# Copying the broadcast root of a norm out of PSUM, summing the last squares apart, and more side work beside the last groups of an FFN

## The chip, the cores and the metric

The kernel runs on one core of one Trainium2 chip. TensorE does the matrix products and writes PSUM banks; VectorE (DVE), ScalarE (ACT) and GpSimd (POOL) do elementwise work; SyncE (SP) issues transfers. The metric is device time in microseconds (us) for one execution. Median of three runs of the kernel before: 2212.97 us (2211.99 to 2215.68).

## The reference

One layer of a streaming encoder over 1024 prompt tokens and 32 sample tokens, width 1024: a gated FFN, two attention mixers, a second gated FFN, each with a norm before it (scaled and shifted) and a norm on its result.

```python
def rmsnorm(x, g):
    y = x * rsqrt(mean(x * x, axis=-1, keepdims=True) + EPS)
    return y * g
def adaln_in(x, g, shift, scale):
    return rmsnorm(x, g) * (1 + scale) + shift
def swiglu(h, w_gate, w_up, w_down):            # 1024 -> 2816 -> 1024
    return (silu(h @ w_gate) * (h @ w_up)) @ w_down
def layer(x, c, ...):
    h = adaln_in(x, gains[0], sh1, sc1)
    x = x + 0.5 * g1 * rmsnorm(swiglu(h, w1_gate, w1_up, w1_down), gains[1])
    h = adaln_in(x, gains[2], sh2, sc2)
    ...                                         # q, k, v = h @ w_in; two attention mixers
    o = concatenate([rmsnorm(oa, gg[:512]), rmsnorm(ob, gg[512:])]) @ w_out
    x = x + g2 * rmsnorm(o, gains[3])
    h = adaln_in(x, gains[4], sh3, sc3)
    x = x + 0.5 * g3 * rmsnorm(swiglu(h, w2_gate, w2_up, w2_down), gains[5])
```

## The kernel before, in words

Activations lie transposed: features on the 128 partitions (8 tiles k), tokens along the free axis, in three token blocks tb: 0 and 1 of 384 tokens, 2 of 256 + 32 = 288 (prompt and sample; scaled by separate coefficients, hence two operations, 256 and 32 wide, per tile). Each f32 product is three matmuls of split operands (`mm3`, L324 to L327: high by high, high by low, low by high), so a product over 8 tiles is 24 matmuls.

**FFN** (`ffn`). The 22 column tiles of the hidden width go in groups of two, x and y. For one block, `up(x)` makes `gate` and `up`, 24 matmuls each, in PSUM; ScalarE applies silu to gate (`sl`, L550), VectorE multiplies it with up (L551) and splits the product (`gg`, L553, L554); then `up(y)`, and `down` adds 4 × 12 `dn` matmuls to `facc`. gate, up, pv, pq and wo share a pool of three banks (`p1`). The first FFN (h1) runs all three blocks in every group but the last three, whose groups run blocks 0 and 1 first and then block 2 alone; the second (h3) begins with two groups of blocks 0 and 1, and then these two of block 2.

**Norm** (`mean_rstd`, `sumsq`). ScalarE squares two tiles at a time (`sq`, L364, four times); GpSimd folds the first two, VectorE the last two (L368, and L370 to add the earlier one); TensorE sums over partitions with `pss` matmuls (L357, one per 128 tokens, after the second and the fourth square); VectorE makes the root from pss (`rv`, `ry`, `rt`, L387 to L391 and L334 to L338, eleven to twelve small operations); TensorE spreads it over the partitions (`pr`, L405, one matmul per 128 tokens). pss and pr are handed out from one bank (`pc`) with other small things.

Two users: `resid` (L454) scales the sublayer's result by pr (L464, VectorE) and adds the old x, loaded as `xr` (L467); `norm_h` (L409) scales x by pr (`n`, L420, VectorE), adds the shift and splits it into `h_hi` (ScalarE, L444) and `h_lo` (L446 VectorE, L448 ScalarE with L449 GpSimd). `between` runs resid and then norm_h for one block. The norm of the mixers' output (`group_norm`) copies pr to SBUF (`rstd`, L1145) before it uses it.

**What sets the order.** These norms are generators in the list `side`; the FFN's `up` calls `step` after the gate's 24 matmuls and after up's 24, which runs some of their pieces in between (`PACE` = 2, in the first group `FAST` = 10). The program made so is then put in order by a list scheduler over all engines: an instruction is placed when its operands and its buffer are there, and each engine executes in the order given. Buffers are handed out in the order of the program. `rstd`, `sl` and a few more take the tag "s" (five buffers), `sq`, `n` and `xr` the tag "h" (five).

Of the kernel before, what the change touches and what calls it, by code (L numbers as in the profile page):

```python
# [33 lines left out]


PACE = 2
FAST = 10
OUTSTEP = 6
ABREAST = 1
# [35 lines left out]
def encoder_step(ctx: ExitStack, tc, x_prompt, x_sample, cache_a_k, cache_a_v, cache_b_k, cache_b_v,  # L75
# [30 lines left out]
    def s_tile(shape, name, dt=F32):  # L106
        return spool.tile(shape, dt, name=name, tag="s")
# [234 lines left out]
    def token_cols(w):  # L342
        return [(c, min(128, w - c)) for c in range(0, w, 128)]

    def sumsq(src, kts, w, bank, ends, fold=True):


        n = len(kts) // 2
        pss = bank("pss")
        cols = token_cols(w)  # L350
        behind = []

        def add_up(sq, first, last):
            halves = (0,) if fold else (0, 1)
            for q in halves:
                for j, (c0, m) in enumerate(cols):
                    te.matmul(pss[:m, j:j + 1], sq[:, q, c0:c0 + m], ones, start=first and j == 0 and q == 0,  # L357
                              stop=last and q == halves[-1], skip_group_check=True)

        acc, first = None, True  # L360
        for c in range(n):
            k = kts[2 * c]
            sq = h_tile([128, 2, 384], "sq")
            ae.activation(sq[:, :, :w], src[:, k:k + 2, :w], AF.Square)  # L364
            if fold:
                e = SQE[c % len(SQE)]
                e = ve if e == "v" else ge
                e.tensor_tensor(sq[:, 0, :w], sq[:, 0, :w], sq[:, 1, :w], op=OP.add)  # L368
                if acc is not None:
                    e.tensor_tensor(sq[:, 0, :w], sq[:, 0, :w], acc[:, 0, :w], op=OP.add)  # L370
                acc = sq
            if behind:
                add_up(*behind.pop())
            if c in ends or not fold:
                behind.append((sq, first, c == n - 1))
                acc, first = None, False
            yield
        add_up(*behind.pop())
        return pss

    def rstd_cols(pss, w, scale):
        cols = token_cols(w)
        v = small.tile([128, 4], F32, name="rv")
        m = cols[-1][1]
        nj = len(cols)
        if m < 128:
            ve.memset(v[:, nj - 1:nj], 1.0)  # L387
            ve.tensor_scalar(v[:, :nj - 1], pss[:, :nj - 1], scale, EPS, op0=OP.mult, op1=OP.add)
            ve.tensor_scalar(v[:m, nj - 1:nj], pss[:m, nj - 1:nj], scale, EPS, op0=OP.mult, op1=OP.add)
        else:  # L390
            ve.tensor_scalar(v[:, :nj], pss[:, :nj], scale, EPS, op0=OP.mult, op1=OP.add)  # L391
        return rsqrt(v[:, :nj], 128, nj)

    waits = [0]

    def mean_rstd(src, kts, w, scale, ends, bank=None):

        bank = bank or pc
        pss = yield from sumsq(src, kts, w, bank, ends)
        y = rstd_cols(pss, w, scale)  # L400
        for _ in range(waits[0]):
            yield
        pr = bank("pr")
        for j, (c0, m) in enumerate(token_cols(w)):
            te.matmul(pr[:, c0:c0 + m], y[:m, j:j + 1].to_broadcast([m, 128]), ident[:m, :m], start=True, stop=True)  # L405
        yield
        return pr

    def norm_h(x, tb, j, H, ahead=0):  # L409
        w = TB[tb][1]  # L410
        r = yield from mean_rstd(x, range(KT), w, 1.0 / D, JN)
        hi, lo = H[tb] = (u_tile(tb, "h_hi", F32R), u_tile(tb, "h_lo", F32R))

        def scaled(c, gated):
            n = h_tile([128, 2, 384], "n")
            if gated:
                for q in range(2):
                    k = 2 * c + q
                    for a, b, st in SEGS[tb]:
                        ve.scalar_tensor_tensor(n[:, q, a:b], x[:, k, a:b], acoef[:, j, st, k:k + 1], r[:, a:b],  # L420
                                                op0=OP.mult, op1=OP.mult)
            else:
                ve.tensor_tensor(n[:, :, :w], x[:, 2 * c:2 * c + 2, :w],
                                 r[:, None, :w].to_broadcast([128, 2, w]), op=OP.mult)
            return n

        ns = [scaled(c, False) for c in range(ahead)]
        if ns:
            yield "ahead"
        for c in range(KT // 2):  # L430
            n = ns[c] if ns else scaled(c, True)
            yield
            for q in range(2):
                k = 2 * c + q
                for a, b, st in SEGS[tb]:
                    sh = modT[:, st, 24 * j + k:24 * j + k + 1]
                    z = n[:, q, a:b]
                    if ns:
                        ac = acoef[:, j, st, k:k + 1]
                        ae.activation(hi[:, k, a:b], z, AF.Identity, bias=sh, scale=ac)  # L440
                        ve.tensor_scalar(z, z, ac, sh, op0=OP.mult, op1=OP.add)
                        (ge if q else ve).tensor_tensor(lo[:, k, a:b], z, hi[:, k, a:b], op=OP.subtract)
                    else:
                        ae.activation(hi[:, k, a:b], z, AF.Identity, bias=sh)  # L444
                        if k % 4 < 3:
                            ve.scalar_tensor_tensor(lo[:, k, a:b], z, sh, hi[:, k, a:b], op0=OP.add, op1=OP.subtract)  # L446
                        else:
                            ae.activation(z, z, AF.Identity, bias=sh)  # L448
                            ge.tensor_tensor(lo[:, k, a:b], z, hi[:, k, a:b], op=OP.subtract)  # L449
            yield  # L450
# [3 lines left out]
    def resid(f, tb, j):  # L454

        w = TB[tb][1]
        r = yield from mean_rstd(f, range(KT), w, 1.0 / D, JR)
        for c in range(KT // 2):
            s = slice(2 * c, 2 * c + 2)
            x = h_tile([128, 2, 384], "xr")  # L460
            dma.dma_start(x[:, :, :w], xs_dram[j][tb][:, s, :])
            for k in (2 * c, 2 * c + 1):
                for a, b, st in SEGS[tb]:
                    ve.scalar_tensor_tensor(f[:, k, a:b], f[:, k, a:b], gcoef[:, j, st, k:k + 1], r[:, a:b],  # L464
                                            op0=OP.mult, op1=OP.mult)
            yield
            (ge if c in POOL_ADDS else ve).tensor_tensor(f[:, s, :], f[:, s, :], x[:, :, :w], op=OP.add)  # L467
            yield
# [56 lines left out]
    def ffn(key, H, F, wg, wu, wd, per_group, key_out, after, beside=lambda ff, tb: None):  # L525
# [10 lines left out]
        for r, (gi, blocks) in enumerate(plan):  # L536
# [3 lines left out]
            def up(ff, tb):  # L540
                need((key, tb))
                w = TB[tb][1]
                hi, lo = H[tb]
                ps = [p1("gate"), p1("up")]
                for s in range(2):
                    for k in range(KT):
                        mm3(ps[s][:, :w], wgu[ff][s], k, hi[:, k, :], lo[:, k, :], k == 0, k == KT - 1)
                    step(FAST if gi == 0 else PACE)
                sl = s_tile([128, 384], "sl")
                ae.activation(sl[:, :w], ps[0][:, :w], AF.Silu)  # L550
                ve.tensor_tensor(sl[:, :w], sl[:, :w], ps[1][:, :w], op=OP.mult)  # L551
                g = g_tile([128, 2, 384], "gg", F32R)
                ae.activation(g[:, 0, :w], sl[:, :w], AF.Copy)  # L553
                ve.tensor_sub(g[:, 1, :w], sl[:, :w], g[:, 0, :w])  # L554
                gs[ff, tb] = g
                beside(ff, tb)
                if late:
                    late.pop()()
# [579 lines left out]
    def group_norm(tb, g):  # L1138
        w = TB[tb][1]
        if OH[tb] is None:  # L1140
            OH[tb] = (u_tile(tb, "o_hi", F32R), u_tile(tb, "o_lo", F32R))
        hi, lo = OH[tb]
        pr = yield from mean_rstd(O[tb], range(4 * g, 4 * g + 4), w, 2.0 / D, JG, p1)
        r = s_tile([128, 384], "rstd")
        ae.activation(r[:, :w], pr[:, :w], AF.Copy)  # L1145
        for c in range(2):
            z = h_tile([128, 2, 384], "z")
            for q in range(2):
                k = 4 * g + 2 * c + q
                ve.scalar_tensor_tensor(z[:, q, :w], O[tb][:, k, :], cst[:, 120 + k:121 + k], r[:, :w],  # L1150
                                        op0=OP.mult, op1=OP.mult)
            yield
            s = slice(4 * g + 2 * c, 4 * g + 2 * c + 2)
            ae.activation(hi[:, s, :], z[:, :, :w], AF.Copy)
            (ge if c in GNP else ve).tensor_tensor(lo[:, s, :], z[:, :, :w], hi[:, s, :], op=OP.subtract)
            yield
# [199 lines left out]
```

## Time and profile before

| | |
|---|---|
| median of the runs | 2212.97 us |
| the profiled execution | 2217.6 us, its span 2215.8 us, mean granted clock 0.984 |
| TensorE busy | 2161.6 us (98%) |
| VectorE, ScalarE, GpSimd busy | 1239.1 (56%), 697.8 (31%), 179.2 us (8%) |
| matmuls | 14012 |
| silu, `sl` (L550) | 132 operations, 60.9 us |
| copy of pr in the group norms (L1145) | 6 operations, 0.41 to 0.49 us each |

A row of a wait names the engine, what waited and for whom, then us in total, times and the longest. A row of a timeline has start, duration, engine, line, operation and, in brackets, the idle time just before and what ended it. A row of a stretch has its bounds, its length, the busy time and instructions (x) of each engine, the granted TensorE clock (1.00 is full), the share of the transfers and GB/s. Times are from the start of the span; the first FFN begins at 45, the work in front of the mixers at 831, the second FFN at 1414.

### The profile page before, as it was taken

The page shows a single profiled execution, that of the slowest core. Times are in us where ns is not written, and L with a number is a line of the kernel's source. Part 1 is how long each engine was busy: PE and PEld are TensorE (multiplying, and loading weights), DVE is VectorE, ACT ScalarE, POOL GpSimd, SP SyncE. Part 2 cuts the span into 40 slices and gives each one's busy share as a digit, 9 for nine tenths or more (in the row PEclk, how much of TensorE's full clock was granted, in tenths as well). Part 3 has the DMA queues.
Part 4 walks back from the last instruction along what each step waited for, and adds up shares of the span by engine and source line. Part 5 has one row for each costly group of instructions (what it writes and reads, how often), then busy time and mean ns, then how long its engine had stood idle before and what let it go on. Part 6 is the DMA issues. An engine that isn't in the chain of part 4 may idle for free.

```text
span 2215.8 us, 33976 instructions
## 1 busy us (share of the span) xinstructions
PE 2161.6 (98%) x14012; PEld 2068.6 (93%) x14012; DVE 1239.1 (56%) x2425; ACT 697.8 (31%) x1450; POOL 179.2 (8%) x281
## 2 busy tenths in 40 slices
PE   6999999999999999899999899999999999999998
PEld 4999999999999999799787589999999999999998
DVE  5788667874333497677444865785333333333336
ACT  4411111111121253576444663542111111111133
POOL 1100000000000023001110313220000000000000
PEclk8999999999999999899999899999999999999999
DMA  9253334434122352111112121424211111111122
GB/s 323 93 153 118 111 96 124 143 101 129 39 66 69 101 184 93 38 39 30 50 30 62 46 77 67 134 86 120 66 58 39 57 39 39 58 38 58 39 69 79
DMA packets 200623, 186.03 MB, mean 84 GB/s; under 512 B 7597, under 2 KB 169813, under 8 KB 199317
## 3 DMA queue, kind: packets, MB, share of 16 engines
q1 hardware_dynamic: 200468, 183.87, 27.1%
q8 instruction: 110, 1.80, 0.3%
q14 instruction: 45, 0.36, 0.1%
HBM read 164.12 MB, written 22.86 MB: 84 GB/s over the span
## 4 chain that ended last, share of the span: by engine, by line
PE 90%; DVE 4%; DMA 3%; ACT 1%; issue 1%; POOL 0%; SPq 0%; ACTq 0%; DVEq 0%; POOLq 0%
PE dn L325 7%; PE dn L326 7%; PE dn L327 7%; PE gate L327 7%; PE gate L326 7%; PE up L327 7%; PE up L326 7%; PE gate L325 7%; PE up L325 7%; PE po L713 3%; PE S L752 2%; PE pq L325 2%; PE pq L327 2%; PE pq L326 2%; DMA raw<-in_w_gate_dram 1%; PE pp L776 1%
## 5 line engine op out<-in xcount | busy, mean ns | idle before, releaser
L326 PE MATMUL gate<-h_lo,w 128*128 128x384 f32 (+1 forms) x1056 | 340.2, 322 | 4.0 <-DVE h_lo L446 4.0
L325 PE MATMUL dn<-gg,w 128*128 128x384 f32 (+1 forms) x1056 | 341.4, 325 | 1.1 <-DVE facc L581 1.0
L581 DVE TENSOR_TENSOR facc<-dn,facc 128x768 f32<-128x768 f32 (+1 forms) x240 | 212.9, 889 | 230.2 <-PE dn L327 229.9
L326 PE MATMUL dn<-gg,w 128*128 128x384 f32 (+1 forms) x1056 | 340.6, 323 | 0.6 <-DVE gg L554 0.6
L325 PE MATMUL gate<-h_hi,w 128*128 128x384 f32 (+1 forms) x1056 | 341.0, 323 | 0.0
L327 PE MATMUL gate<-h_hi,w 128*128 128x384 f32 (+1 forms) x1056 | 340.4, 322 | 0.0
L325 PE MATMUL up<-h_hi,w 128*128 128x384 f32 (+1 forms) x1056 | 340.2, 322 | 0.0
L326 PE MATMUL up<-h_lo,w 128*128 128x384 f32 (+1 forms) x1056 | 340.0, 322 | 0.0
L327 PE MATMUL dn<-gg,w 128*128 128x384 f32 (+1 forms) x1056 | 340.0, 322 | 0.0
L327 PE MATMUL up<-h_hi,w 128*128 128x384 f32 (+1 forms) x1056 | 339.9, 322 | 0.0
L304 DVE TENSOR_TENSOR w<-raw,w 128x1024 fp32r<-128x1024 f32 x187 | 231.5, 1246 | 150.5 <-ACT w L303 150.3
L303 ACT ACTIVATE w<-raw 128x1024 fp32r<-128x1024 f32 x187 | 195.7, 1056 | 266.1 <-PE dn L327 103.5
L550 ACT ACTIVATE sl<-gate 128x384 f32<-128x384 f32 (+1 forms) x132 | 60.9, 462 | 563.9 <-PE gate L327 560.9
L551 DVE TENSOR_TENSOR sl<-sl,up 128x384 f32<-128x384 f32 (+1 forms) x132 | 68.5, 519 | 292.1 <-PE up L327 286.1
L326 PEld LDWEIGHTS gate<-h_lo,w 128*128 128x128 f32 x1056 | 198.6, 188 | 4.6 <-DVE h_lo L446 4.6
L325 PEld LDWEIGHTS dn<-gg,w 128*128 128x128 f32 x1056 | 199.2, 189 | 1.6 <-DVE facc L581 1.2
L326 PEld LDWEIGHTS dn<-gg,w 128*128 128x128 f32 x1056 | 199.2, 189 | 1.0 <-DVE gg L554 0.9
L327 PEld LDWEIGHTS dn<-gg,w 128*128 128x128 f32 x1056 | 199.1, 189 | 0.0
L325 PEld LDWEIGHTS gate<-h_hi,w 128*128 128x128 f32 x1056 | 198.7, 188 | 0.1
L327 PEld LDWEIGHTS gate<-h_hi,w 128*128 128x128 f32 x1056 | 198.7, 188 | 0.0
L327 PEld LDWEIGHTS up<-h_hi,w 128*128 128x128 f32 x1056 | 198.7, 188 | 0.0
L325 PEld LDWEIGHTS up<-h_hi,w 128*128 128x128 f32 x1056 | 198.5, 188 | 0.0
(224 smaller groups left out, 3367.4 us busy)
## 6 DMA issues: line engine op xcount, KB each, us to landing
raw<-in_w_mod_dram SPq DMA_DIRECT2D x56, 512.0 KB, 4.0
raw<-in_w_gate_dram SPq DMA_DIRECT2D x54, 512.0 KB, 4.0
raw<-in_w_up_dram SPq DMA_DIRECT2D x54, 512.0 KB, 4.7
raw<-in_w_down_dram SPq DMA_DIRECT2D x54, 512.0 KB, 4.5
raw<-in_w_in_dram SPq DMA_DIRECT2D x18, 512.0 KB, 4.3
wm<-in_w_mod_dram SPq DMA_DIRECT2D x8, 1024.0 KB, 7.4
raw<-in_w_out_dram SPq DMA_DIRECT2D x13, 512.0 KB, 4.5
xr<-xs SPq DMA_DIRECT2D x16, 384.0 KB, 3.5
```

Source lines behind the costliest of these rows:

```text
L303: ae.activation(w[:, 0], r, AF.Copy)
L304: ve.tensor_sub(w[:, 1], r, w[:, 0])
L325: te.matmul(ps, w[:, 0, k], hi, start=start, stop=False)
L326: te.matmul(ps, w[:, 0, k], lo, start=False, stop=False)
L327: te.matmul(ps, w[:, 1, k], hi, start=False, stop=stop)
L550: ae.activation(sl[:, :w], ps[0][:, :w], AF.Silu)
L551: ve.tensor_tensor(sl[:, :w], sl[:, :w], ps[1][:, :w], op=OP.mult)
L581: ve.tensor_tensor(o, ps[:, :, :w], o, op=OP.add)
L713: te.matmul(po[64 * h:64 * h + 64, :n], vsl(j, h, kn), PT(h, j, kn), start=j == 0, stop=j == nt - 1)
L752: te.matmul(S[:, c:ce], self.T[:, h, :], KQ[:, 0, 128 * k0 + c:128 * k0 + ce], start=True, stop=True)
L776: te.transpose(pp[:, j - j0, :], P[:, 128 * j:128 * j + 128], ident)
```

## The change

Three things. `mean_rstd` copies pr into an SBUF tile `rstd` on ScalarE (all norms but the very first; the group norms had that copy), and hands that out, so that pr's bank is free after the copy; `sumsq` asks for the bank of pss only with the first sum. For block 2, in resid and in all norm_h but the first sublayer's, the last square is not folded: TensorE sums its two halves with twice as many matmuls, next to those of the third (`ends` is (2, 3)). Where a group runs block 2 alone, `step` gets `BEHIND` = 5 instead of 2.

```diff
+BEHIND = 5
...
-    def sumsq(src, kts, w, bank, ends, fold=True):
+    def sumsq(src, kts, w, bank, ends, fold=True, apart=False):
         n = len(kts) // 2
-        pss = bank("pss")
         cols = token_cols(w)
-        behind = []
+        behind, banks = [], []
         def add_up(sq, first, last):
-            halves = (0,) if fold else (0, 1)
+            halves = (0,) if fold and not (apart and last) else (0, 1)
+            if first:
+                banks.append(bank("pss"))
+            pss = banks[0]
...
-            if fold:
+            if fold and not (apart and c == n - 1):
...
-        return pss
+        return banks.pop()
...
-    def mean_rstd(src, kts, w, scale, ends, bank=None):
+    def mean_rstd(src, kts, w, scale, ends, bank=None, apart=False, copied=True):
         bank = bank or pc
-        pss = yield from sumsq(src, kts, w, bank, ends)
+        if apart:
+            ends = (len(kts) // 2 - 2, len(kts) // 2 - 1)
+        pss = yield from sumsq(src, kts, w, bank, ends, apart=apart)
         y = rstd_cols(pss, w, scale)
+        del pss
...
+        if copied:
+            r = s_tile([128, 384], "rstd")
+            ae.activation(r[:, :w], pr[:, :w], AF.Copy)
+            pr = r
         yield
         return pr
...
     def norm_h(x, tb, j, H, ahead=0):
-        r = yield from mean_rstd(x, range(KT), w, 1.0 / D, JN)
+        r = yield from mean_rstd(x, range(KT), w, 1.0 / D, JN, apart=tb == 2 and j > 0, copied=tb > 0 or j > 0)
...
     def resid(f, tb, j):
-        r = yield from mean_rstd(f, range(KT), w, 1.0 / D, JR)
+        r = yield from mean_rstd(f, range(KT), w, 1.0 / D, JR, apart=tb == 2)
...
-                    step(FAST if gi == 0 else PACE)
+                    step(FAST if gi == 0 else BEHIND if blocks == (2,) else PACE)
...
-        pr = yield from mean_rstd(O[tb], range(4 * g, 4 * g + 4), w, 2.0 / D, JG, p1)
-        r = s_tile([128, 384], "rstd")
-        ae.activation(r[:, :w], pr[:, :w], AF.Copy)
+        r = yield from mean_rstd(O[tb], range(4 * g, 4 * g + 4), w, 2.0 / D, JG, p1)
```

How it moves instructions, at three places; the lines of the kernel after are 1 to 10 higher (mm3 L326 to L328, pss L360, sq L367, pr L411, rstd L414, h_hi L454, sl L560, gg L563, pv L679 to L681).

First place: TensorE at the start of the second FFN, where the second gate of the first group ends. Before, up follows the gate, and the sum of block 1's second norm stands amid it:

```order
7531 L327 MATMUL up<-h_hi,w 128x384
7532 L325 MATMUL up<-h_hi,w 128x384
7533 L357 MATMUL pss<-ones,sq 128x1 x6
7534 L326 MATMUL up<-h_lo,w 128x384
7535 L327 MATMUL up<-h_hi,w 128x384
7536 L325 MATMUL up<-h_hi,w 128x384
```

Its pr comes later, amid dn:

```order
7547 L327 MATMUL dn<-gg,w 128x384
7548 L325 MATMUL dn<-gg,w 128x384 x2
7549 L405 MATMUL pr<-ident,ry 128x128 x3
7550 L326 MATMUL dn<-gg,w 128x384
7551 L327 MATMUL dn<-gg,w 128x384
```

After (block 1's second norm is the first pss with its pr, block 2's first norm the second):

```order
7505 L328 MATMUL gate<-h_hi,w 128x384
7506 L360 MATMUL pss<-ones,sq 128x1 x6
7507 L411 MATMUL pr<-ident,ry 128x128 x3
7508 L360 MATMUL pss<-ones,sq 128x1 x2
7509 L360 MATMUL pss<-ones,sq 32x1
7510 L360 MATMUL pss<-ones,sq 128x1 x2
7511 L360 MATMUL pss<-ones,sq 32x1
7512 L360 MATMUL pss<-ones,sq 128x1 x2
7513 L360 MATMUL pss<-ones,sq 32x1
7514 L411 MATMUL pr<-ident,ry 128x128 x2
7515 L411 MATMUL pr<-ident,ry 128x32
7516 L326 MATMUL up<-h_hi,w 128x384
```

Both norms' sums and roots now stand between the second gate and its up, with no matmul of the FFN between a pss and its pr.

Second place: ScalarE in the same stretch. Before, with the table load for silu ahead of the first:

```order
840 L550 ACT_TABLE_LOAD
841 L550 ACTIVATE sl<-gate 128x384
842 L364 ACTIVATE sq<-fo 128x768 x4
843 L553 ACTIVATE gg<-sl 128x384
844 L550 ACTIVATE sl<-gate 128x384
845 L553 ACTIVATE gg<-sl 128x384
846 L364 ACTIVATE sq<-fo 128x2x288
```

After:

```order
856 L367 ACTIVATE sq<-fo 128x2x288 x2
857 L414 ACTIVATE rstd<-pr 128x288
858 L560 ACT_TABLE_LOAD
859 L560 ACTIVATE sl<-gate 128x384
860 L563 ACTIVATE gg<-sl 128x384
861 L367 ACTIVATE sq<-fo 128x2x288 x4
862 L304 ACTIVATE w<-raw 128x1024
863 L414 ACTIVATE rstd<-pr 128x288
864 L560 ACTIVATE sl<-gate 128x384 x2
```

The first silu stands behind block 2's first copy, the second and third behind its second.

Third place: TensorE in front of the mixers, at the second norm of block 2. Before, after the products with the v weights (pv) of block 1:

```order
5154 L670 MATMUL pv<-w,h_hi 128x256
5155 L671 MATMUL pv<-w,h_lo 128x256
5156 L357 MATMUL pss<-ones,sq 128x1 x2
5157 L357 MATMUL pss<-ones,sq 32x1
5158 L357 MATMUL pss<-ones,sq 128x1 x2
5159 L357 MATMUL pss<-ones,sq 32x1
5160 L405 MATMUL pr<-ident,ry 128x128 x2
5161 L405 MATMUL pr<-ident,ry 128x32
5162 L669 MATMUL pv<-w,h_hi 128x256
```

After, the sums:

```order
5066 L360 MATMUL pss<-ones,sq 128x1 x2
5067 L360 MATMUL pss<-ones,sq 32x1
5068 L681 MATMUL pv<-w,h_lo 128x256
5069 L326 MATMUL pq<-h_hi,w 128x384
5070 L327 MATMUL pq<-h_lo,w 128x384
```

and the spreading, 35 large matmuls (24 pq, 11 pv) later:

```order
5101 L681 MATMUL pv<-w,h_lo 128x256
5102 L679 MATMUL pv<-w,h_hi 128x256
5103 L411 MATMUL pr<-ident,ry 128x128 x2
5104 L411 MATMUL pr<-ident,ry 128x32
5105 L680 MATMUL pv<-w,h_hi 128x256
```

The norm of block 2 moved forward among the products of blocks 0 and 1. From some sixty matmuls further on, TensorE's order is the old one until the mixers' second half.

## Prediction

> **What bounds the kernel now.** I read the page first (busy shares, chain), then the waits of TensorE, then the timelines around them, and last the order of the changed kernel's instructions.
>
> ```profile
> span 2215.8 us, 33976 instructions
> ...
> PE 2161.6 (98%) x14012; PEld 2068.6 (93%) x14012; DVE 1239.1 (56%) x2425; ACT 697.8 (31%) x1450; POOL 179.2 (8%) x281
> ...
> PE 90%; DVE 4%; DMA 3%; ACT 1%; issue 1%; POOL 0%; SPq 0%; ACTq 0%; DVEq 0%; POOLq 0%
> ```
>
> TensorE works 98% of the span, and the chain that ended last is 90% TensorE. The change leaves the large matmuls alone, so it can only move the 54.2 us in which TensorE is idle, and the clock that follows them. The waits of TensorE, grouped (line waited for: us in total, times, longest), that belong to the norms and to the FFN beside them:
>
> ```profile
> PE pr L405 <- DVE ry L338: 4.8, 2, 2.4
> ...
> PE gate L326 <- DVE h_lo L446: 4.0, 2, 2.1
> ...
> PE pk L1057 <- DVE n L420: 1.9, 1, 1.9
> ...
> PE pv L669 <- ACT h_hi L444: 1.1, 1, 1.1
> PE dn L325 <- DVE facc L581: 1.0, 1, 1.0
> ...
> PE dn L326 <- DVE gg L554: 0.6, 1, 0.6
> PE pss L357 <- DVE sq L370: 0.6, 1, 0.6
> ```
>
> That is 14.0 us in nine waits, one of the pr waits (2.4) being a group norm's. More cannot be won here, but for the clock.
>
> **The gain: the norms of the last block in front of the mixers.** The end of block 2's norm there, on TensorE (start, us, idle before it):
>
> ```profile
> 885.28 0.51 PE L357 MATMUL pss<-ones,sq 128*128 128x1 f32 x4
> 888.24 1.75 PE L405 MATMUL pr<-ident,ry 128*128 128x128 f32 x6 [2.44 <-DVE ry L338]
> 891.11 0.58 PE L669 MATMUL pv<-w,h_hi 128*128 128x256 f32 x1 [1.11 <-ACT h_hi L444]
> ...
> 894.66 1.08 PE L1057 MATMUL pk<-ident,vt 128*128 128x128 f32 x4 [1.91 <-DVE n L420]
> ```
>
> Nothing stands between the last sum (pss) and the broadcast of the root (pr), so TensorE waits out the eleven small VectorE operations: 2.44 us. This row is my price of "pss and pr side by side". 2.44 + 1.11 + 1.91 = 5.46 us idle. The clock behind it (stretch, us, ..., PEclk before the last two columns), with two other places where TensorE had waited 1.9 and 2.1 us for h_lo:
>
> ```profile
> 880.00:887.30 7.30, 5.80 (x51) 5.67 (x49) 4.58 (x13) 3.06 (x6) 2.79 (x4) 1.00 0.39 162
> 887.30:897.50 10.20, 6.24 (x26) 5.31 (x27) 8.06 (x31) 6.86 (x22) 1.58 (x4) 0.50 0.00 0
> ...
> 75.00:78.40 3.40, 3.40 (x13) 3.40 (x12) 3.40 (x5) 1.26 (x2) 2.05 (x3) 0.51 0.02 5
> ...
> 1443.60:1447.00 3.40, 3.40 (x12) 3.40 (x11) 3.40 (x5) 0.68 (x1) 2.09 (x3) 0.50 0.02 5
> ```
>
> In the second row 6.24 us of matmuls ran at half clock: 3.1 us lost. What a matmul takes in a full stream: 24 of up at 384 columns, 24 at 288, 72 of pv:
>
> ```profile
> 1419.04:1423.20 4.16, 4.16 (x24) 4.00 (x24) 0.00 (x0) 1.00 0.45 137
> ...
> 805.20:808.40 3.20, 3.20 (x24) 3.12 (x24) 0.00 (x0) 1.00 0.00 0
> ...
> 875.83:884.45 8.62, 8.62 (x72) 8.58 (x72) 0.74 (x2) 1.00 0.30 122
> ```
>
> So 0.173, 0.133 and 0.120 us each. In the changed order (third place above) 11 pv and 24 pq matmuls (384 columns) stand between this pss and its pr, 5.5 us, and 64 pv (7.7 us) before block 2's first projection. The 5.5 cover 2.44, the 7.7 cover what follows pr, today's 1.11 and 1.91 and a copy. So the stall goes whole: **−8.6 us**. What is late next is nothing: TensorE's order joins the old one soon behind. If the cover failed, 8.6 would stay.
>
> **The direct cost.** 14 copies of pr to SBUF on ScalarE, 4 by 3 more pss matmuls, four folds less. Durations (ns min/median/max):
>
> ```profile
> L464 DVE SCALAR_TENSOR_TENSOR fo<-fo,gcoef,pr x32: 242/542/614, 1371.7 to 1466.3; 128x384 f32<-128x384 f32 x16, 128x256 f32<-128x256 f32 x8, 128x32 f32<-128x32 f32 x8
> L420 DVE SCALAR_TENSOR_TENSOR n<-fo,acoef,pr x32: 242/544/615, 1392.5 to 1490.7; 128x384 f32<-128x384 f32 x16, 128x256 f32<-128x256 f32 x8, 128x32 f32<-128x32 f32 x8
> L1145 ACT ACTIVATE rstd<-pr x6: 410/485/490, 1236.5 to 1354.1; 128x384 f32<-128x384 f32 x4, 128x288 f32<-128x288 f32 x2
> ...
> L550 ACT ACTIVATE sl<-gate x132: 388/491/495, 60.3 to 2185.6; 128x384 f32<-128x384 f32 x88, 128x288 f32<-128x288 f32 x44
> ...
> L550 ACT ACT_TABLE_LOAD  x1: 1283/1283/1283, 1417.9 to 1417.9; - x1
> ```
>
> 14 × 0.485 = 6.8 us on an engine busy 31%: nothing by itself, as is the VectorE scaling, whose source alone changes (whether it reads SBUF faster I leave at 0). What counts is what now stands behind a copy.
>
> **The loss: silu behind the copies.** rstd and sl share one pool of five buffers (tag "s"), and the side work's rstd is asked for ahead of the sl of the same column. In the changed order every sl that has norms beside it stands on ScalarE behind the copy; so `up` of the second column, which needs the bank that this silu empties (gate and up take three), stands behind pr on TensorE. Cover that lay between pss and pr, and behind pr, is gone. Three places.
>
> (a) Start of the second FFN (1414). On TensorE now, pr of block 1's first norm, the end of the second gate, and the next sum:
>
> ```profile
> 1415.74 0.83 PE L405 MATMUL pr<-ident,ry 128*128 128x128 f32 x6
> ...
> 1427.18 0.34 PE L327 MATMUL gate<-h_hi,w 128*128 128x384 f32 x1
> ...
> 1431.55 0.47 PE L357 MATMUL pss<-ones,sq 128*128 128x1 f32 x3 [0.62 <-DVE sq L370]
> ```
>
> On VectorE that norm's scaling, the second norm's, and a copy of facc amid its operations:
>
> ```profile
> 1419.02 4.28 DVE L464 SCALAR_TENSOR_TENSOR fo<-fo,gcoef,pr 128x384 f32<-128x384 f32 x8
> ...
> 1437.51 4.29 DVE L420 SCALAR_TENSOR_TENSOR n<-fo,acoef,pr 128x384 f32<-128x384 f32 x8 [1.57 <-PE pr L405]
> ...
> 1442.79 0.94 DVE L579 COPY facc<-dn 128x768 f32<-128x768 f32 x1
> ```
>
> On ScalarE the last square of block 2:
>
> ```profile
> 1448.69 0.69 ACT L364 ACTIVATE sq<-fo 128x576 f32<-128x576 f32 x1 [0.86 <-DVE h_lo L446]
> ```
>
> In the changed order the second gate is followed by pss, pr, pss, pr and only then by up. The gate still ends at about 1427.4. From the first scaling to the next sum it is 12.5 us today (1431.55 − 1419.02). The pr comes 18 matmuls (3.1 us) later, ends at 1419.7, and with 0.49 of copy the scaling starts at 1420.2, 1.2 later: sum at 1432.7. Then 0.8 (pss, by 0.51 for four), 2.44, 0.83 (pr) and 0.49 (copy): 1437.3. The squares of block 2 wait for buffers: today the last ends 11.9 us behind the first n (1449.4 − 1437.5), with two copies of facc between that don't stand there in the changed order; so I take 10: 1447.3. Then pss 1.2, 2.44, pr 0.83, copy 0.41, table load 1.28 and silu 0.49: up starts at 1454.0. TensorE loses 26.6 less the 3.4 us of pss and pr that it did before too: 23.2. Half a microsecond follows for a bank, and block 2's second norm, with pss and pr side by side again: 2.44 + 0.41 + 0.49 = 3.3. In all 27.0, against 2.1 + 0.6 before: **+24.3 us**. Bounds: three side-by-side pairs with copy and silu alone, 3 × 3.3 = 10 (+7); or the 11.9 uncut and 5 more in VectorE's queue, 34 (+31).
>
> (b) The last groups of the first FFN (783 to 830). Four norms now run in a row there. From the first norm's last pss to the last pr TensorE has 88 gate, 72 up and 96 dn matmuls. At 0.133 us (288 columns; 42 of the dn have 384) these make 36 us. The chain is 4 × (2.44 + 0.83) + 3 × 0.485 + 2 × 12.5 (resid, as above) + 8 (norm: scaling 4.29, square 0.7, folds, an estimate from the rows of (a)) = 48. So at least 12 us idle; two pairs stand side by side, and cover in one place doesn't serve another: 14, against 1.0 + 0.6 before: **+12.4 us** (bounds +5, two pairs, and +17).
>
> (c) Start of the first FFN. On TensorE the last sum, and up of the second column:
>
> ```profile
> 60.44 0.72 PE L357 MATMUL pss<-ones,sq 128*128 128x1 f32 x6
> ...
> 62.50 0.33 PE L325 MATMUL up<-h_hi,w 128*128 128x384 f32 x1
> ```
>
> On ScalarE the silu of the first gate, and two copies of weights:
>
> ```profile
> 60.28 0.49 ACT L550 ACTIVATE sl<-gate 128x384 f32<-128x384 f32 x1 [0.48 <-PE gate L327]
> ...
> 63.29 1.05 ACT L303 ACTIVATE w<-raw 128x1024 fp32r<-128x1024 f32 x1
> 64.66 1.06 ACT L303 ACTIVATE w<-raw 128x1024 fp32r<-128x1024 f32 x1 [0.32 <-DMA raw<-in_w_up_dram]
> ```
>
> The first silu, now at 60.28, comes behind both weight copies and rstd: 64.66 + 1.06 + 0.49 + 0.49 = 66.7 instead of 62.5 for up: 4.2 less pr 0.8, 3.4. Behind it the wait for h_lo shrinks little (1.6), one pair side by side with copy and silu takes 3.4, and up once more behind the scalings some 2: 10.4 against 1.9: **+8.5 us** (bounds +3 and +11).
>
> **The clock.** After each of the waits of 1.9 and 2.1 us, 3.4 us ran at half clock, 1.7 lost. Some eight new waits are that long or longer: 13.6 at most, 0 at least; many lie close together, so I take three, **+5 us**. The Trainium skill, "TensorE: Matmul & The Clock Gate", Part 1, "What's actually happening", lets the clock fall only after an idle window of about 3.4 us; the rows above, with 1.9 and 2.1 us of idle time, don't agree. By that rule only (a)'s two long waits would cost anything, about 3 us instead of 5.
>
> **Sum.** 24.3 + 12.4 + 8.5 − 8.6 + 5 = +41.6 us. The profiled execution took 2217.6 us (its span and 1.8 around it): 2259.2. That execution lies 4.6 us, 0.2%, above the median of the runs, and so I forecast 2254.6.
>
> **Rivals.**
> 1. Faster. The bank of pr is free 4 us earlier, the stall of 8.6 goes, and silu and pr find cover after all. The Trainium skill, "PSUM — Partial Sum Buffer", "Summary: rules for kernel authors", says to evacuate promptly, which is this. For it: the third place of the order, 35 matmuls between. Against: the first place, none. 2212.97 − 8.6 = 2204. It decides where the new waits stay under the old 6.2 us of those places plus 8.6, some 15. Chance 0.05.
> 2. Only the side-by-side pairs cost: six (three, two, one) with copy and silu, 6 × 3.4 = 20.4, less 6.2 and 8.6: +5.6, 2219. The chain would have to keep up with TensorE; 48 against 36 speaks against it. Chance 0.1.
> 3. No effect: new waits of 10 to 19 us cancel the gain, or silu gets its buffer in time: 2209 to 2217. Chance 0.05.
> 4. The forecast, 2222 to 2277: chance 0.8; its upper end has all upper bounds (31 + 17 + 11 − 8.6 + 13.6 = 64).
>
> A measurement tells 0.2%, 4.4 us, from no change. Slower by that: 0.89; within: 0.06; faster: 0.05. Range 2219 to 2277.
>
> **What would show it.** Right: the 2.44 before pr at 888 and the half clock behind it are gone; TensorE idle by over 15 us between 1425 and 1460, with pr waiting for ry twice; three or more waits of pr for ry of about 2.4 in 783 to 830; silu directly behind rstd in ScalarE's timeline. Wrong: if up of the second column begins within 5 us of the second gate's end, (a) falls, and with it more than half of the sum.

## The result, and the profile after

The change costs 73 us. Median 2287.06 us (2285.35 to 2287.52) against 2213.64 us before on the same chip; ratio 1.0331, 95% interval 1.0314 to 1.0347. The direction was forecast, the size was not: 2254.6 was predicted, with 2277 as the upper end.

The page of the kernel after:

```profile
span 2285.0 us, 34036 instructions
...
PE 2181.2 (95%) x14036; PEld 2088.0 (91%) x14036; DVE 1248.3 (55%) x2421; ACT 703.3 (31%) x1464; POOL 182.6 (8%) x281
...
PEclk8999999999999979999999999879999999999999
```

The span grew by 69.2 us, less than the median, as the profiled execution of the kernel before lay some 4 us above its median. TensorE is idle for 103.8 us instead of 54.2 (+49.6) and busy for 19.6 us more, although only 12 small matmuls came in (24 records: the trace has two for each of them, as it has x6 for three of pr). Most of the 19.6 is matmuls at half clock. What TensorE waits for, in total us, times, longest:

```profile
PE pr L411 <- DVE ry L339: 23.7, 9, 4.6
PE pss L360 <- DVE sq L373: 15.4, 2, 12.3
PE pss L360 <- POOL sq L373: 10.2, 4, 5.4
...
PE up L326 <- ACT sl L560: 9.5, 8, 2.3
```

Before, pr waited for ry twice; now nine times, and `up` waits for silu eight times, which it never did. By comparing when the same matmul runs in both traces, the growth falls to five stretches:

| stretch | forecast, clock apart | measured, clock in it | of it idle |
|---|---|---|---|
| start of the first FFN (c) | +8.5 | +8.6 | +6.3 |
| its last groups (b) | +12.4 | +39.9 | +23.4 |
| last norm before the mixers | −8.6 (clock in it) | −7.6 | −5.5 |
| mixers | 0 | −4.2 | |
| start of the second FFN (a) | +24.3 | +33.0 | +25.5 |

Stretch (a) on TensorE's timeline, all its rows with a wait of over 0.5 us:

```profile
1469.65 2.72 PE L360 MATMUL pss<-ones,sq 128*128 128x1 f32 x12 [5.38 <-POOL sq L373]
1474.68 1.62 PE L411 MATMUL pr<-ident,ry 128*128 128x128 f32 x6 [2.31 <-DVE ry L339]
1488.58 3.44 PE L360 MATMUL pss<-ones,sq 128*128 128x1 f32 x18 [12.29 <-DVE sq L373]
1494.39 1.75 PE L411 MATMUL pr<-ident,ry 128*128 128x128 f32 x6 [2.36 <-DVE ry L339]
1498.44 0.69 PE L326 MATMUL up<-h_hi,w 128*128 128x384 f32 x1 [2.30 <-ACT sl L560]
...
1514.27 1.75 PE L411 MATMUL pr<-ident,ry 128*128 128x128 f32 x6 [2.72 <-DVE ry L339]
1516.90 0.69 PE L326 MATMUL up<-h_hi,w 128*128 128x384 f32 x1 [0.88 <-ACT sl L560]
```

This is the chain that was read off the order: two norms one after the other, with nothing of the FFN in between. ScalarE's rows show the silu behind copy and table load:

```profile
1496.18 0.41 ACT L414 ACTIVATE rstd<-pr 128x288 f32<-128x288 f32 x1 [9.82 <-PE pr L411]
1496.61 1.28 ACT L560 ACT_TABLE_LOAD   x1
1497.90 0.49 ACT L560 ACTIVATE sl<-gate 128x384 f32<-128x384 f32 x1
```

And (b), the waits from 800 on (two come before, of 1.54 us for silu's multiplication L561 and of 2.78 us for the split L564, both on VectorE):

```profile
805.13 1.62 PE L411 MATMUL pr<-ident,ry 128*128 128x128 f32 x6 [4.62 <-DVE ry L339]
807.63 0.60 PE L326 MATMUL up<-h_hi,w 128*128 128x288 f32 x1 [0.88 <-ACT sl L560]
818.28 0.83 PE L360 MATMUL pss<-ones,sq 128*128 128x1 f32 x6 [1.05 <-POOL sq L373]
822.26 1.41 PE L360 MATMUL pss<-ones,sq 128*128 128x1 f32 x6 [3.15 <-DVE sq L373]
825.98 1.62 PE L411 MATMUL pr<-ident,ry 128*128 128x128 f32 x6 [2.31 <-DVE ry L339]
...
836.03 0.40 PE L326 MATMUL gate<-h_hi,w 128*128 128x288 f32 x1 [2.12 <-DVE sl L561]
851.71 1.62 PE L411 MATMUL pr<-ident,ry 128*128 128x128 f32 x6 [3.81 <-DVE ry L339]
854.21 0.61 PE L326 MATMUL up<-h_hi,w 128*128 128x288 f32 x1 [0.88 <-ACT sl L560]
```

The three waits of pr are 4.62, 2.31 and 3.81 us, where the chain of the forecast had 2.44 for each; before the sums, 1.05 and 3.15 are idle, and a gate waits 2.1 us for the multiplication in VectorE's queue. VectorE at the first of these waits: two operations on weights (L305) stand between the first steps of the root.

```profile
800.86 0.15 DVE L394 TENSOR_SCALAR rv<-pss 128x3 f32<-128x3 f32 x1
800.92 1.22 DVE L305 TENSOR_TENSOR w<-raw,w 128x1024 fp32r<-128x1024 f32 x1
802.05 0.16 DVE L335 TENSOR_SCALAR ry<-rv 128x3 int32<-128x3 int32 x1
802.12 1.22 DVE L305 TENSOR_TENSOR w<-raw,w 128x1024 fp32r<-128x1024 f32 x1
803.26 0.16 DVE L337 TENSOR_TENSOR rt<-ry 128x3 f32<-128x3 f32 x1
```

The granted clock, all stretches at half clock in (b) and (a), with their sum:

```profile
792.00:795.40 3.40, 3.40 (x15) 3.40 (x13) 3.40 (x4) 0.00 (x0) 0.53 (x1) 0.50 0.98 398
802.20:812.40 10.20, 6.39 (x26) 6.13 (x27) 7.59 (x20) 5.09 (x11) 1.01 (x1) 0.50 0.36 104
819.30:833.00 13.70, 7.55 (x31) 7.23 (x32) 10.54 (x23) 0.88 (x3) 2.34 (x2) 0.50 0.62 193
836.40:839.80 3.40, 3.40 (x17) 3.40 (x16) 2.20 (x4) 2.92 (x5) 1.94 (x2) 0.50 0.41 173
850.00:860.20 10.20, 7.61 (x31) 7.34 (x32) 7.81 (x15) 6.30 (x13) 1.05 (x1) 0.50 0.34 104
1467.80:1501.90 34.10, 12.99 (x53) 12.18 (x54) 23.15 (x58) 11.23 (x19) 9.50 (x9) 0.50 0.20 69
1512.20:1522.40 10.20, 7.25 (x23) 6.92 (x24) 7.51 (x29) 6.34 (x21) 1.35 (x2) 0.50 0.18 52
sum 85.20, PE 48.59 PEld 46.60 DVE 62.20 ACT 32.75 POOL 17.72; mean PE 6.94 PEld 6.66 DVE 8.89 ACT 4.68 POOL 2.53
```

48.6 us of TensorE's work ran at half clock, so about 24 us were lost there: 14 in (b), 10 in (a). The kernel before had no such stretch in (b) and two of 3.4 us in (a), the one from 1443.6 and this one:

```profile
1433.40:1436.80 3.40, 3.40 (x13) 3.40 (x12) 1.89 (x8) 1.10 (x2) 0.80 (x1) 0.50 0.00 0
```

They cost it 3.4 us. So the change adds some 21 us in (a) and (b), counted in the same way, and 1 us in (c). Forecast for all: 5.

One more thing stands in the rows of VectorE's scaling, now with rstd from SBUF. One group of them, and the two GpSimd operations beside it:

```profile
778.49 4.84 DVE L474 SCALAR_TENSOR_TENSOR facc<-facc,gcoef,rstd 128x384 f32<-128x384 f32 x6
...
783.71 2.52 DVE L474 SCALAR_TENSOR_TENSOR facc<-facc,gcoef,rstd 128x384 f32<-128x384 f32 x2
```

```profile
780.77 2.14 POOL L477 TENSOR_TENSOR facc<-facc,xr 128x768 f32<-128x768 f32 x1 [17.49 <-DVE facc L474]
783.46 1.83 POOL L477 TENSOR_TENSOR facc<-facc,xr 128x768 f32<-128x768 f32 x1 [0.55 <-ACT w L304]
```

Eight scalings took 7.36 us instead of 4.28. In (b) the same happens again right in front of the gate that waits 2.12 us for the multiplication L561, which VectorE does behind these eight:

```profile
828.16 7.46 DVE L474 SCALAR_TENSOR_TENSOR facc<-facc,gcoef,rstd 128x384 f32<-128x384 f32 x8 [2.32 <-ACT rstd L414]
```

Over the whole kernel 14 of the 88 scalings of 384 columns whose third operand is rstd took 1.15 to 2.21 us, each beside a GpSimd operation that ran for all but the last 0.4 of it. 20 others overlap a GpSimd addition or subtraction and took at most 0.64. What divides them is who was first: the GpSimd operation began before the scaling in 13 of the 14, and 0.01 us after it in one; it began 0.02 to 0.61 us after the scaling in all the 20. With pr in PSUM, before, 23 of 72 ran beside GpSimd operations, and none took over 0.62.

### The profile page after: what moved, and what is told of

Same layout as the page of the kernel before. It is cut to its first block, busy times and chain, and to the rows that moved or that the text cites. A ratio compares the mean times of both kernels' runs of the same rounds, so it can differ in the third digit from the quotient of the medians.

```text
span 2285.0 us, 34036 instructions
## 1 busy us (share of the span) xinstructions
PE 2181.2 (95%) x14036; PEld 2088.0 (91%) x14036; DVE 1248.3 (55%) x2421; ACT 703.3 (31%) x1464; POOL 182.6 (8%) x281
## 5 line engine op out<-in xcount | busy, mean ns | idle before, releaser
L326 PE MATMUL up<-h_hi,w 128*128 128x384 f32 (+1 forms) x1056 | 346.9, 329 | 9.5 <-ACT sl L560 9.5
L326 PE MATMUL gate<-h_hi,w 128*128 128x384 f32 (+1 forms) x1056 | 341.2, 323 | 5.1 <-DVE sl L561 3.7
L327 PE MATMUL up<-h_lo,w 128*128 128x384 f32 (+1 forms) x1056 | 345.1, 327 | 0.0
L328 PE MATMUL up<-h_hi,w 128*128 128x384 f32 (+1 forms) x1056 | 344.5, 326 | 0.0
L328 PE MATMUL gate<-h_hi,w 128*128 128x384 f32 (+1 forms) x1056 | 340.3, 322 | 0.0
L326 PE MATMUL dn<-gg,w 128*128 128x384 f32 (+1 forms) x1056 | 340.2, 324 | 0.0
L328 PE MATMUL dn<-gg,w 128*128 128x384 f32 (+1 forms) x1056 | 339.4, 322 | 0.0
L305 DVE TENSOR_TENSOR w<-raw,w 128x1024 fp32r<-128x1024 f32 x187 | 232.0, 1248 | 153.5 <-ACT w L304 151.5
L560 ACT ACTIVATE sl<-gate 128x384 f32<-128x384 f32 (+1 forms) x132 | 60.7, 462 | 558.5 <-PE gate L328 555.7
L561 DVE TENSOR_TENSOR sl<-sl,up 128x384 f32<-128x384 f32 (+1 forms) x132 | 68.5, 519 | 297.1 <-PE up L328 291.2
L326 PEld LDWEIGHTS up<-h_hi,w 128*128 128x128 f32 x1056 | 203.2, 192 | 11.2 <-ACT sl L560 11.2
L326 PEld LDWEIGHTS gate<-h_hi,w 128*128 128x128 f32 x1056 | 199.1, 189 | 5.8 <-DVE sl L561 4.1
L327 PEld LDWEIGHTS up<-h_lo,w 128*128 128x128 f32 x1056 | 203.4, 193 | 0.0
L328 PEld LDWEIGHTS up<-h_hi,w 128*128 128x128 f32 x1056 | 203.4, 193 | 0.0
L327 PEld LDWEIGHTS dn<-gg,w 128*128 128x128 f32 x1056 | 198.7, 188 | 3.1 <-DVE gg L564 3.1
L328 PEld LDWEIGHTS gate<-h_hi,w 128*128 128x128 f32 x1056 | 199.0, 188 | 0.0
L326 PEld LDWEIGHTS dn<-gg,w 128*128 128x128 f32 x1056 | 198.5, 188 | 0.3 <-DVE facc L591 0.3
```

The source lines that it names most:

```text
L305: ve.tensor_sub(w[:, 1], r, w[:, 0])
L326: te.matmul(ps, w[:, 0, k], hi, start=start, stop=False)
L327: te.matmul(ps, w[:, 0, k], lo, start=False, stop=False)
L328: te.matmul(ps, w[:, 1, k], hi, start=False, stop=stop)
```

## The experiments

Differences are to the kernel before, run on the same chip, with the ratio's 95% interval.

**1. A tag of their own for the copies** (own32).

```diff
-    spool = ctx.enter_context(tc.tile_pool(name="spool", bufs=5))
+    spool = ctx.enter_context(tc.tile_pool(name="spool", bufs=3))
...
-            r = s_tile([128, 384], "rstd")
+            r = spool.tile([128, 384], F32, name="rstd", tag="rs", bufs=2)
```

> The changed kernel, but the copies of pr (rstd) take a tag of their own with 2 buffers, and tag s keeps 3; copies, separate sums and side work stay. Theory (silu held behind the copies because rstd and sl share buffers that are handed out in program order): the order shows cover between pss and pr again at all places of the two FFNs, and none at the last norm before the mixers; so all three losses go, and the gain there too: 2213, between 2208 and 2219. Rival (the copies, the extra sums or the earlier side work cost the time themselves): 2250 to 2287.

Measured: 2242.82 us, +24.6 (1.0111, 1.0096 to 1.0126). Between the two theories. Two thirds of the loss go with the shared tag, and TensorE's order has its cover back, as expected: pr waits for ry twice again. But 25 us stay that the theory had not. Their waits, and the scaling in front of the largest:

```profile
PE gate L327 <- DVE h_lo L456: 7.3, 2, 4.1
PE pss L360 <- POOL sq L373: 6.6, 4, 3.2
PE pr L411 <- DVE ry L339: 4.8, 2, 2.5
...
PE dn L326 <- DVE facc L591: 4.4, 2, 4.3
PE pss L360 <- DVE sq L373: 3.8, 3, 3.3
```

```profile
838.11 7.45 DVE L474 SCALAR_TENSOR_TENSOR facc<-facc,gcoef,rstd 128x384 f32<-128x384 f32 x8
845.48 0.74 DVE L591 TENSOR_TENSOR facc<-dn,facc 128x576 f32<-128x576 f32 x1
```

```profile
840.39 2.14 POOL L477 TENSOR_TENSOR facc<-facc,xr 128x768 f32<-128x768 f32 x1 [18.15 <-DVE facc L474]
843.03 2.11 POOL L477 TENSOR_TENSOR facc<-facc,xr 128x768 f32<-128x768 f32 x1 [0.49 <-DVE facc L474]
```

The scalings take 7.45 us instead of 4.28, the facc addition behind them empties its bank late, and dn waits 4.3 us for it. That led to the theory of experiment 5, called the port theory from here on: a VectorE operation with both tensors in SBUF is held up by an operation of GpSimd.

**2. The copy made, but not used** (unused).

```diff
             ae.activation(r[:, :w], pr[:, :w], AF.Copy)
-            pr = r
+            if bank is p1:
+                pr = r
```

(The bank is p1 in the group norms alone, which keep their use of it.)

> The changed kernel, but outside the group norms VectorE reads pr from PSUM as before: the copy is still made, from the shared tag s, and nobody uses it. Theory of the shared buffers: the order is that of the changed kernel, silu still stands behind the copies, so nearly all the loss stays: 2275 to 2287 (some nine copies of 0.49 us off the chain). Rival (the loss is the longer chain through the copy, or the scaling from SBUF): under 2240, towards 2214.

Measured: 2279.77 us, +61.7 (1.0278, 1.0263 to 1.0293). TensorE's order is that of the changed kernel, place by place, and 62 of 73 us stay although outside the group norms nobody uses a copy: silu only stands behind it in ScalarE's queue. So the longer chain through the copy isn't the main cause, and with experiment 1 the shared tag is. The missing 12 us are more than nine copies (4.4): the rest fits the scalings by pr, which all take at most 0.62 here.

**3. Copies between the first FFN and the mixers alone** (h1end).

```diff
-        ..., JN, apart=tb == 2 and j > 0, copied=tb > 0 or j > 0)
+        ..., JN, apart=tb == 2 and j > 0, copied=j == 1)
...
-        ..., JR, apart=tb == 2)
+        ..., JR, apart=tb == 2, copied=j == 0)
```

> The changed kernel with the copies only in the norms between the first FFN and the mixers (4 + 2 norms); the norms at the start of the two FFNs read pr from PSUM. Theory: the places add up: +41 us (end of the first FFN) and -11 (last norm before the mixers) alone: 2240 to 2246, or 4 us less if the small gain in the mixers also comes from there. Rival (the places hang together, one long chain from the first FFN on): under 2225 or over 2260.

Measured: 2246.9 us, +29.1 (1.0131, 1.0114 to 1.0148); the kernel before took 2218.0 on this chip, so the expected difference is 26 to 32. The places add up. In its trace (b) costs 41 us, the norm before the mixers gives back 9, and the mixers 4.

**4. Side work as before** (beh2).

```diff
-BEHIND = 5
+BEHIND = 2
```

> The changed kernel with 2 steps of side work as before instead of 5 beside the last groups. Theory: the silu is held all the same; the order shows 5.1 and 5.6 us of matmuls between pss and pr at two of the four norms at the end of the first FFN, where the changed kernel has 0 and 1.6, so some 6 to 20 us of that place's 41 come back with the clock: 2267 to 2281. Rival (the side work is the cause of that place): 2245 or less.

Measured: 2275.52 us, +58.3 (1.0263, 1.0245 to 1.0281), 15 us less than with 5. The steps beside the last groups add to (b), but they aren't its cause. TensorE's idle time there is hardly shorter, +20 us over the kernel before instead of +23. What comes back is mainly the clock: instead of five stretches with 28.4 us of work there is one, long but mostly idle.

```profile
808.50:832.40 23.90, 9.22 (x38) 8.82 (x39) 19.60 (x37) 9.22 (x17) 7.89 (x7) 0.50 0.41 123
```

The 9.2 us of work in it lost 4.6 us, where (b) of the changed kernel lost 14.

**5. Own tag, copies not used** (unused32): the edits of 1 and 2 together.

> As the kernel with the copies' own 2 buffers, and 3 for the rest, but VectorE reads pr from PSUM, and nobody uses the copies outside the group norms. Same order of TensorE. New theory (VectorE's scaling, with both operands in SBUF, waits for the end of GpSimd's operations: in that kernel 16 of 88 scalings took 1.2 to 2.2 us instead of 0.54, all beside a GpSimd operation, and with pr in PSUM none): at least 10 of its 25 us over the kernel before go: +0 to +14. Rival (three buffers for the rest, or the separate sums, cost them): +18 to +27.

Measured: 2225.77 us, +10.0 (1.0045, 1.003 to 1.0061). 15 of the 25 us go. So the port theory, which put it at 10 or more, holds. TensorE's order has the same cover as in experiment 1, and the copies are still made; where VectorE reads from differs. Its scalings in the two residuals:

```profile
L475 DVE SCALAR_TENSOR_TENSOR facc<-facc,gcoef,pr x32: 241/542/614, 773.5 to 887.1; 128x384 f32<-128x384 f32 x16, 128x256 f32<-128x256 f32 x8, 128x32 f32<-128x32 f32 x8
...
L475 DVE SCALAR_TENSOR_TENSOR fo<-fo,gcoef,pr x32: 239/542/617, 1377.8 to 1473.4; 128x384 f32<-128x384 f32 x16, 128x256 f32<-128x256 f32 x8, 128x32 f32<-128x32 f32 x8
```

and in experiment 1:

```profile
L474 DVE SCALAR_TENSOR_TENSOR facc<-facc,gcoef,rstd x32: 238/608/2204, 776.3 to 895.8; 128x384 f32<-128x384 f32 x16, 128x256 f32<-128x256 f32 x8, 128x32 f32<-128x32 f32 x8
...
L474 DVE SCALAR_TENSOR_TENSOR fo<-fo,gcoef,rstd x32: 239/608/2208, 1388.9 to 1493.4; 128x384 f32<-128x384 f32 x16, 128x256 f32<-128x256 f32 x8, 128x32 f32<-128x32 f32 x8
```

The longest (third number, ns) is 2208 from SBUF and 617 from PSUM. The wait of dn for facc is 1.6 us here instead of 4.3.

**6. No copies** (nocopy): `copied=False` in resid and norm_h, all else of the change kept.

> The changed kernel without the copies outside the group norms: bank of pss taken with the first sum, separate last squares of block 2 and 5 steps beside the last groups stay. Both theories (shared buffers, port): no loss is left, the order keeps the cover of before and the stall before the mixers: -4 to +5 us against the kernel before. Rival (separate sums or side work cost by themselves): +8 or more.

Measured: 2220.97 us, +4.0 (1.0018, 1.0009 to 1.0028). The separate sums, the later request for the bank and the side work bring nothing here, and cost about 4 us at most; the stall of 2.45, 1.11 and 1.91 us before the mixers is there as it was. So the gain of the changed kernel at that place came with the copies.

**7. Three buffers, nothing else** (s3): the kernel before with `bufs=3` in spool.

> The kernel before with 3 instead of 5 buffers of tag s (silu, small copies, bias rows). Theory that the port made the remaining 25 us of the kernel with the copies' own buffers: 0 to +5. Rival (three buffers for silu and the bias rows): +12 to +25.

Measured: 2215.49 us, −0.2 (0.9999, 0.9988 to 1.001). Fewer buffers for silu cost nothing in the kernel before, so it is unlikely that they made experiment 1's rest.

**8. Silu written ahead of the side work** (sil).

```diff
                         mm3(ps[s][:, :w], wgu[ff][s], k, ...)
+                    if s == 0:
+                        sl = s_tile([128, 384], "sl")
+                        ae.activation(sl[:, :w], ps[0][:, :w], AF.Silu)
                     step(...)
-                sl = s_tile([128, 384], "sl")
-                ae.activation(sl[:, :w], ps[0][:, :w], AF.Silu)
```

> The changed kernel with silu written right behind the gate's matmuls, ahead of the side work's steps, so that its buffer is asked for before that of a copy. Theory of the shared buffers in program order: the order has cover again at the start of the first FFN (6.4 and 7.6 us between pss and pr) and at one norm more at its end (8.1, 0.5, 0, 0) and at the third of the second FFN's start (0, 0, 5.0): some 9 of (c) and 10 to 25 of (a) and (b) come back: +38 to +55 against the kernel before. Rival (the place of silu in the program doesn't matter): +65 to +75.

Measured: 2269.68 us, +52.1 (1.0235, 1.0218 to 1.0252), 21 us less than the changed kernel, with the same buffers. The place of the silu in the program, which decides who asks for a buffer first, does matter. Most silus still stand behind a copy, some behind an earlier one: at the start of the second FFN the first up now waits for block 1's second norm and no longer for block 2's first, and TensorE idles there for 12.8 us more than before the change instead of 25.5.

**9. The free space to the squares** (s3h6): experiment 7, and `bufs=6` instead of 5 in hpool.

> The kernel before with 3 instead of 5 buffers of tag s, which cost nothing, and the space given to tag h (squares, scaled rows, loads of the residual): 6 instead of 5. If the squares of the next norm wait for these buffers on the path, the wait for h_lo at the starts of the FFNs (1.9 and 2.1 us) shrinks: -2 to -8 us against the kernel before; if VectorE's queue holds them, 0 +- 3.

Measured: 2208.66 us, −6.2 (0.9972, 0.9962 to 0.9982): the fastest of all, faster than both kernels. The waits of the gates for h_lo, 4.0 us before, are nearly gone:

```profile
PE gate L326 <- POOL h_lo L449: 0.6, 1, 0.6
```

**10. Group norms without their copy** (gnpsum): the kernel before, with z scaled from PSUM.

> The kernel before with the copy of pr in the group norms taken away: VectorE scales from PSUM. Port theory: its two scalings of 1.8 and 2.2 us beside GpSimd (at 1239 and 1341) fall to 0.54 to 0.62; as TensorE waits there for other things, -3 to +1 us. Rival (the bank of three that pr holds longer holds up the scores): +3 or more.

Measured: 2215.45 us, −0.4 (0.9998, 0.9989 to 1.0007). No difference, although the chain that ended last in the kernel before runs through the scaling at 1239. Without its delay TensorE waits for other things: 2.8 us from 1233 to 1262 in both traces.

## Why the prediction was right and wrong

**Right: the mechanism of the main loss.** Copies and silu share the tag s; the silu waits behind the copies, and up behind silu; sums and roots stand side by side. Experiments 1, 2 and 8 show it from three sides. (a)'s idle time was forecast at +24.3 us and is +25.5, with waits of 5.4, 2.3, 12.3, 2.4 and 2.3 us where 5.3, 2.4, some 10, 2.4 and 2.2 were worked out. There is some luck in it: the 5.4 has a part of the long scalings in it that the forecast didn't know (experiment 2, without them, waits 3.8 there, and 11.5 for the 12.3). In (c) the luck is larger: +8.6 with the clock in it agrees with +8.5 without it, but the idle time is only +6.3.

**Right: the gain before the mixers.** The 2.44, 1.11 and 1.91 us are gone, −7.6 us against −8.6. But it is no gain of a free bank: experiment 2, where VectorE reads pr out of its bank as before, has the same gain in its trace, −7.3. The reading that is left is that TensorE idles in (b), the norms run on, and block 2's chain stands that much earlier. Experiment 3 has the loss of (b) alone and the gain; experiment 6 has no loss and no gain there, and experiment 1 has lost most of the loss and the gain too.

**Wrong: the clock, +5.** This is the largest miss: about 24 us were lost at half clock in (a) and (b), 21 more than before, and 1 more in (c). I counted single windows of 3.4 us behind single waits, and took three of eight as net. In the trace one wait follows another before the clock is up again, and the windows join: 34.1 us from 1467.8, 13.7 us from 819.3. The 13.6 us that were to be the upper bound were none. No run was made to test this count. Experiment 4 comes near it: nearly the same idle time in (b), and 4.6 us lost at half clock instead of 14. The wait before the clock also needn't be long: in the kernel before, the 3.4 us from 1433.4 followed an idle time of 0.62 us between two groups of small sums.

**Wrong: (b), +12.4 with a bound of +17.** Measured +23.4 us idle. The chain of 48 us against 36 us of cover gave 12 and was set at 14; the pairs were priced at 2.44 and are 4.62, 3.81 and 2.31 us: in two of the three the eleven small operations stand in VectorE's queue between others, and that queue was left out of the price. So were FFN operations that wait in it: 1.54, 2.78 and 2.12 us of TensorE's idle time are for the multiplication and the split behind silu. Part is the next point: experiment 2, without the long scalings, has none of the waits for the multiplication, and 2.1 us less idle time in (b).

**Wrong: the scaling from SBUF, priced at 0.** The prediction quoted the row of L1145 and left the scaling at 0. The row of its user, z of the group norms, which was not quoted, had the answer: three numbers of 512, 606 and 2162 ns, with a maximum that no scaling from PSUM reaches. The Trainium skill has the rule, in "SBUF — State Buffer", "Who interferes with whom": a VectorE instruction with two inputs in SBUF contends with a GpSimd instruction that reads SBUF, the ports that they share are an exclusive lock, and issue order decides which of them blocks. By it a scaling of facc or x times rstd can be blocked, and one with pr in PSUM is not; experiment 5 agrees, with 2.2 against at most 0.62 us, and 15 us of device time. The trace of the changed kernel agrees too, with GpSimd first in 13 of its 14 slow scalings and second in the 20 others. In the changed kernel this is worth no more than the 12 us between it and experiment 2, of which nine copies on the chain are 4.4.

**Open.** The mixers give back 4 us in the traces of the changed kernel and of experiment 3. It isn't shorter waits: from 1225 to 1405 TensorE's idle time is 6.6 us before and 7.6 after, while 11.0 and 7.3 us were lost at half clock. The traces of experiments 7 and 10, kernels without this change, take 2.7 us less there too (that of experiment 9 does not), so most of the 4 us need not be the change's. Of the 10 us of experiment 5, 4 are those of experiment 6; the other 6, with copies that nobody uses, were not taken apart. Whether the sums apart or the steps cost those 4 was not tested either.

## What to carry to other kernels

A copy that frees a bank early isn't free because its engine is idle: ask which pool its target comes from, and who asks that pool next. Before an operand is moved from PSUM to SBUF, look at what GpSimd does beside its reader: the maximum, not the median, of the same operation elsewhere in the trace shows the price. When waits come in a row, price the clock over the whole stretch: at most half speed for all the work from the first wait to the end of the last. (a) came near that; in (b) it was 41 of 78 us.

## What the runs showed of the hardware

A scaling of 128x384 with both tensors in SBUF took 2.2 us beside a GpSimd addition of 2.1 us that had begun before it, and at most 0.62 with one of them in PSUM. TensorE's clock stayed at half for 34.1 us in a row in which it was busy for 13.0. It went down for 3.4 us behind single waits of 1.9 and 2.1 us, and once (1433.4, before) behind 0.62 us among twelve records of small sums.
